# A two-layer hybrid backbone on one core: convolution taps issued during the attention of layer 1, second group's queries during the first, modulation vectors of layer 0 one place earlier

## The chip, the core and the metric

The kernel runs on one core of a Trainium2 chip as one program. Each engine works through its own list of instructions in order: TensorE (PE, matrix products and transposes), VectorE (DVE), ScalarE (ACT), GpSimd (POOL), and SyncE (SP), which issues the transfers. The metric is the device time of one execution in microseconds. Three runs of the kernel before took 1968.97, 1981.49 and 1981.51 us; the median is 1981.49 us.

## The reference, cut to what matters

Two layers; each has a token-mixing part and an MLP, with 512 latent tokens and 256 context tokens, width 1024, all in fp32. In the mixing part one projection feeds three mixers and 24 blocks of gates:

```python
ul_pool, ul_q, ul_k, ul_v, ul_conv, ul_gate = _split_in(hl @ w_in[i] + b_in[i])
ol = _latent_attention(ql, kl, vl, kc, vc, attn_sink[i])   # 8 heads in 2 groups, +-128 tokens and all context keys
y_conv = _conv_module(...)  # GLU -> depthwise conv, 31 taps -> LayerNorm -> swish -> product
g_pool, g_attn, g_conv = jnp.split(sigmoid(gates), N_BRANCH, axis=-1)
y = (g_pool * y_pool + g_attn * y_attn + g_conv * y_conv) @ w_out
```

The modulation vectors (shift, scale and gate, s = 0 to 5 of each layer) are `silu(c) @ w_mod + b_mod`. The context stream is updated in layer 0 only; in layer 1 the context gives keys and values and nothing else, so `has_ctx` is false there.

## The kernel before, in words

Every operand of a product is held as a high and a low part (`wh`/`wl`, `actah`/`actal`), and three products make one fp32-like product: L156 for stationary weights. A weight unit is 128x512: a transfer, a cast on ACT (L134) and a subtraction (L137) on POOL or DVE.

`w_phase` (L560) is the mixing part of one layer. Its work on PE comes from two sources that are merged while the program is written:

- `other = gated_steps()` is a generator of dense work: eight attention gates (stored to `sgd`), then for each of eight blocks of channels the pool gate with the pool branch's product and the conv gate with the conv branch's product; the sum of both goes to DRAM (`mfd`). `branch_steps` gives nothing (`None`) until its branch is in `mixed`. A gate's tanh is on ACT (L611), a branch's gating on DVE (L621).
- Work with chains of dependences (values, pool products, conv norm, blocks of attention) is put in a heap by `later(columns, steps)` and comes up when that many more columns of PE work were issued. `cover(columns)` issues that many columns of `other`. `pace(steps, every)` issues one step of a third stream each so many columns. When `other` gives `None`, the heap is drained with nothing between its pieces; `flush()` does the same.

Layer 1 in the kernel before: values, keys and the first group's queries; then `conv` (L312) puts 62 DVE taps (two halves of 128 channels by 31 taps, 512 tokens each) in one block, accumulating in one 1024-wide PSUM tile; then `cover(118000)`; then the pool products (L722) and `conv_norm` (L328: transposes, LayerNorm and swish in two blocks of 256 tokens), each waiting for cover; then attention, eight blocks (`items`, L756) of a group and 128 queries. A block makes scores on PE, the row maximum (L511, L512) on DVE, exp (L515) on ACT, scaling (L423) on DVE and one quarter on another engine, transposes on PE, high and low parts (`pth` L445 on ACT, `ptl` L446 on DVE) and the products with V. The second group's queries are made between block 4 and block 5. At the end the rest of `other` and the output loop (`fin`) run.

PSUM: `psa` (2 banks) is shared by the branch products, the attention outputs `po`, pool products and conv norm; `psg` (2 banks) by gates and projections; `pss` by the scores (two tiles of two banks).

Layer 0 has the same order with both streams, `cover(145000)` under the taps, and one pace in the mixing part: the modulation vector s=2, one step each 10000 columns, whose weights arrive in `mg` tiles. The vectors s=3 and s=4 are paced through the output loop, and what is left is issued after it with nothing beside it (L836). A step has four products L185; the last one adds a row on DVE (L222) and, for s=3 and s=4, makes two PE transposes (L234).

Of the kernel before, what the change touches and what calls it, by code (L numbers as in the profile page):

```python
# [10 lines left out]
F32 = mybir.dt.float32  # L11
F32R = mybir.dt.float32r
AF = mybir.ActivationFunctionType
ALU = mybir.AluOpType
# [55 lines left out]
W_CONV1 = 118000  # L70
# [7 lines left out]
def backbone(ctx: ExitStack, tc: tile.TileContext, I: dict, out: bass.AP):  # L78
# [233 lines left out]
    def conv(pool, psum, cvec, gls, st):  # L312

        n = TL if st == 0 else TC
        ps = psum.tile([P, 1024], F32, tag="S", name=uid("cp"))
        accs = []
        for j in range(2):
            gl, run = gls[j, st], ps[:, j * 512:j * 512 + n]
            acc = pool.tile([P, n], F32, tag=f"ca{st}", name=uid("ca"), bufs=2)
            V.tensor_scalar(out=run, in0=gl[:, 0:n], scalar1=cvec[:, j, 0:1], scalar2=cvec[:, j, 31:32],  # L320
                            op0=ALU.mult, op1=ALU.add)
            for k in range(1, CK):
                V.scalar_tensor_tensor(out=run if k < CK - 1 else acc, in0=gl[:, k:k + n],
                                       scalar=cvec[:, j, k:k + 1], in1=run, op0=ALU.mult, op1=ALU.add)
            accs.append(acc)
        return accs

    def conv_norm(pool, scratch, cvec, accs, st, dst):  # L328
# [4 lines left out]
        for b0 in range(0, n, 256):  # L333
            pt, pb = bank(), bank()
# [12 lines left out]
            yield W_CN  # L347
            for j in range(2):
# [62 lines left out]
    def softmax_pv(pp, pss, g, Pt, vtiles, negm, sums, V_, sink, dst, qsl):  # L411
# [42 lines left out]
        t1 = pp.tile([64, 4, P], F32, tag="t1", name=uid("t1"), bufs=1)  # L454
        S.copy(t1, po[64:128, :].rearrange("p (a q) -> p a q", a=4))
        ot = pp.tile([P, 2, P], F32, tag="ot", name=uid("ot"), bufs=2)
# [6 lines left out]
    def attn_ctx(pp, pss, g, nb, Q, KH, KL, V_, nsink, sink, dst):  # L463
# [3 lines left out]
        for a in range(4):  # L467
            o = s[:, a * 256:(a + 1) * 256]
            T.matmul(o, Q[a][:, qsl], KH[g][:, CS], start=True, stop=False)
            T.matmul(o, Q[a][:, qsl], KL[g][:, CS], start=False, stop=True)  # L470
# [15 lines left out]
    def attn_lat(pp, pss, g, n, Q, KH, KL, V_, nsink, sink, dst, masks):  # L486
# [10 lines left out]
        for a in range(4):  # L497
            s = pss.tile([P, 1024], F32, tag="S", name=uid("S"))
            q = Q[a][:, qsl]
# [60 lines left out]
    def w_phase(i, A, B, has_ctx, pre, todo):  # L560
# [5 lines left out]
        with ExitStack() as ph:  # L566
# [8 lines left out]
            mg = ph.enter_context(tc.tile_pool(name=f"mg{i}", bufs=4 if todo else 6, reuse_waits="tile"))  # L575
            sgd = [dram.tile([P, W], F32, tag=f"sg{i}{m}", name=uid("sgd")) for m in range(KD)]
            mfd = [dram.tile([P, W], F32, tag=f"mf{i}{m}", name=uid("mfd")) for m in range(KD)]
            mix = ph.enter_context(ExitStack())
# [14 lines left out]
            if todo:  # L593
                pace((x for s in todo for x in mod_steps(i, s, 0, D, lambda: mg.tile(
                    [P, W], F32, tag="sg", name=uid("wm"))[:, :512])), 10000, 20000)
# [28 lines left out]
            def gated_steps():  # L624
                for m in range(KD):
                    g = yield from gate_steps(m, 1)
                    nc.sync.dma_start(out=sgd[m], in_=g)

                w, d, e, ahead = {}, {}, {}, 0 if todo else 2
                for m in range(ahead):  # L630
                    d[m] = yield from gate_steps(m, 0)
                for m in range(KD + 1):
                    if m + ahead < KD:
                        d[m + ahead] = yield from gate_steps(m + ahead, 0)
                    if m < KD:
                        w[m] = weight_a(I["wbr"][i, m][:, 0:4 * P])
                        yield from branch_steps(w[m], (0, 1), 0, d[m], outs_all, side["bank"])
                    if m:
                        e = yield from gate_steps(m - 1, 2)
                        yield from branch_steps(w.pop(m - 1), (2, 3), 2, e, outs_all, side["bank"])  # L640
# [3 lines left out]
            mixed, side = set(), {"bank": psa}  # L644
# [11 lines left out]
            masks = kv.tile([P, 2, P], F32R, tag="masks", name=uid("masks"))  # L656
            KH = [kv.tile([P, TA], F32R, tag=f"kh{g}", name=uid("kh")) for g in range(NKV)]
            KL = [kv.tile([P, TA], F32R, tag=f"kl{g}", name=uid("kl")) for g in range(NKV)]
            V_ = kv.tile([P, 6, NKV, P], F32R, tag="V", name=uid("V"))

            def evac(ps, t):
                qf = kv.tile([P, TA], F32, tag="qf", name=uid("qf"))
                for st, p_ in enumerate(ps):
                    sl = (LS, CS)[st]
                    S.activation(qf[:, sl], p_, AF.Identity, bias=b_in[:, t:t + 1])
                return qf

            def query(Q, g, jj, temp):
                t = T_Q + 2 * g + jj
                qf = evac(proj(t, LC), t)  # L670
                rope(temp, qf, cs)
                for par in range(2):
# [3 lines left out]
                    V.tensor_copy(q[r, :W], qf[r, :W])  # L676
                    V.tensor_tensor(out=q[ro, :W], in0=qf[r, :W], in1=q[r, :W].bitcast(F32),
                                    op=ALU.subtract)
# [12 lines left out]
            vf = evac(proj(T_V, [LS, CS]), T_V)  # L691
# [14 lines left out]
            kf = evac(proj(T_K, [LS, CS]), T_K)  # L706
# [8 lines left out]
            Q = [kv.tile([P, W], F32R, tag=f"q{a}", name=uid("q")) for a in range(4)]  # L715
# [26 lines left out]
            accs = {st: conv(cp, pss, cvec, gls, st) for st, _ in outs_all}  # L742
            cover((W_CONV0 if has_ctx else W_CONV1) - W_PC)
            for wait in pool_products():
                cover(wait)
            mixed.add(0)
            cover(W_PC)
            flush()
            for st, _ in outs_all:
                for wait in conv_norm(cp, scratch, cvec, accs[st], st, B):  # L750
                    cover(wait)
            mixed.add(2)
            t12.close()
            pp = mix.enter_context(tc.tile_pool(name=f"pp{i}", bufs=1, side="right", reuse_waits="tile"))

            def items():  # L756
                for g in range(NKV):
                    if g:
                        Q[:] = [kv.tile([P, W], F32R, tag=f"q{a}", name=uid("q")) for a in range(4)]
                        for jj in range(2):  # L760
                            query(Q, g, jj, pp.tile([P, TL], F32, tag="rt", name=uid("rt"), bufs=1))
                    for n in range(4):
                        yield attn_lat(pp, pss, g, n, Q, KH, KL, V_, nsink, sink, B, masks)
# [49 lines left out]
            mixed.add(4)  # L813
            mix.close()
            if todo:
                for _ in pe["pace"]:
                    pass
            pace(None, 0)
# [3 lines left out]
            side["bank"] = psg  # L822
            if todo:
                pace((x for s in (3, 4) for x in mod_steps(i, s, 0, D, lambda: fin.tile(
                    [P, D], F32, tag="wm", name=uid("wm"), bufs=4))), 9000)
            drain(other)
            for m in range(KD):
# [4 lines left out]
                nc.sync.dma_start(out=d, in_=mfd[m])  # L832
# [236 lines left out]
    with tc.manual_schedule(engines={mybir.EngineType.PE}):  # L1069
# [159 lines left out]
```

## Time and profile before

| what | value |
|---|---|
| median of three runs | 1981.49 us |
| the profiled execution | 1975.67 us, its span 1973.9 us |
| PE busy | 1848.6 us, 94% of the span |
| DVE, POOL, ACT busy | 1200.3, 771.6, 730.8 us |
| mixing part of layer 1 | about 1232 to 1550 us |

A stretch of the windows view gives, for each engine, how much of that stretch it was busy, and the granted clock of TensorE as a share of full speed. A row of the waits view gives how long an engine stood idle before one line's instructions, and what ended it.

### The profile page before, as it was taken

What the parts mean: (1) busy time and instruction counts of PE and PEld (TensorE: products, weight loads), DVE (VectorE), ACT (ScalarE), POOL (GpSimd) and SP (SyncE); (2) the same over time, 40 slices, a digit from 0 to 9 for tenths busy, and PEclk for the clock granted to TensorE, in tenths of its full rate; (3) what the DMA queues carried; (4) which work ended last, traced back from release to release, by engine and by line L of the source; (5) the groups of instructions that cost most, each with busy time, mean ns of one, the idle gap of its engine ahead of it and who ended that gap; (6) DMA issues with size and microseconds to landing.
All of it is one profiled execution on the core that took longest, in us unless ns stands there. A gap on an engine that the chain in (4) does not pass through costs nothing. (4 is left out here: it accounts for less than half of the span.)

```text
span 1973.9 us, 27007 instructions
## 1 busy us (share of the span) xinstructions
PE 1848.6 (94%) x9910; PEld 1548.4 (78%) x9910; DVE 1200.3 (61%) x2067; ACT 730.8 (37%) x1359; POOL 771.6 (39%) x629
## 2 busy tenths in 40 slices
PE   6999899899899999999999988999988989999997
PEld 4788788787678888888788868777866768888886
DVE  6489655654478946865533584786575784333356
ACT  4432255353234422233133344434444354333331
POOL 3653432322434422222122546664342554333343
PEclk8999999999999999999999989999999989999999
DMA  8523111114865434464422423141212753332341
GB/s 304 176 90 118 62 59 46 53 44 154 281 219 190 161 112 133 155 213 143 146 62 86 129 96 105 61 149 63 69 65 96 260 189 118 96 96 86 107 129 43
DMA packets 117557, 244.94 MB, mean 124 GB/s; under 512 B 14608, under 2 KB 16944, under 8 KB 117424
## 3 DMA queue, kind: packets, MB, share of 16 engines
q1 hardware_dynamic: 117424, 243.21, 38.0%
q8 instruction: 78, 1.28, 0.3%
q14 instruction: 55, 0.45, 0.1%
HBM read 223.20 MB, written 19.96 MB: 123 GB/s over the span
## 5 line engine op out<-in xcount | busy, mean ns | idle before, releaser
L137 POOL TENSOR_TENSOR wl<-raw,wh 128x512 fp32r<-128x512 f32 x371 | 516.7, 1405 | 783.6 <-ACT wh L134 698.9
L134 ACT CAST wh<-raw 128x512 fp32r<-128x512 f32 x506 | 310.8, 621 | 596.0 <-PE ps L167 292.1
L156 PE MATMUL ps<-actbh,wh 128*128 128x512 f32 (+1 forms) x1016 | 353.4, 348 | 14.3 <-DVE sg L621 6.9
L156 PE MATMUL ps<-actbl,wh 128*128 128x512 f32 (+1 forms) x1016 | 348.3, 343 | 3.1 <-POOL actbl L251 3.1
L156 PE MATMUL ps<-actbh,wl 128*128 128x512 f32 (+1 forms) x1016 | 347.8, 342 | 2.7 <-DVE rs L261 1.3
L156 PE MATMUL ps<-actah,wh 128*128 128x512 f32 (+1 forms) x928 | 331.4, 357 | 13.7 <-ACT actah L248 4.7
L156 PE MATMUL ps<-actal,wh 128*128 128x512 f32 (+1 forms) x928 | 327.4, 353 | 3.3 <-DVE actal L1097 1.9
L156 PE MATMUL ps<-actah,wl 128*128 128x512 f32 (+1 forms) x928 | 326.9, 352 | 0.4 <-POOL wl L137 0.3
L156 PEld LDWEIGHTS ps<-actbh,wh 128*128 128x128 f32 x1016 | 194.5, 191 | 45.2 <-DVE sg L621 10.0
L156 PEld LDWEIGHTS ps<-actbh,wl 128*128 128x128 f32 x1016 | 194.4, 191 | 25.6 <-DVE wl L137 2.4
L156 PEld LDWEIGHTS ps<-actbl,wh 128*128 128x128 f32 x1016 | 194.6, 192 | 23.3 <-POOL actbl L251 3.8
L156 PEld LDWEIGHTS ps<-actah,wh 128*128 128x128 f32 x928 | 177.5, 191 | 43.8 <-ACT actah L248 5.1
L156 PEld LDWEIGHTS ps<-actal,wh 128*128 128x128 f32 x928 | 177.6, 191 | 25.6 <-DVE actal L1097 2.2
L156 PEld LDWEIGHTS ps<-actah,wl 128*128 128x128 f32 x928 | 177.4, 191 | 24.2 <-POOL wl L137 1.0
L165 PE MATMUL ps<-wh,actah 128*128 128x512 f32 x480 | 192.6, 401 | 2.2 <-DVE acc L977 2.0
L167 PE MATMUL ps<-wh,actal 128*128 128x512 f32 x480 | 190.5, 397 | 3.5 <-DVE actal L251 3.5
L166 PE MATMUL ps<-wl,actah 128*128 128x512 f32 x480 | 190.1, 396 | 0.0
L137 DVE TENSOR_TENSOR wl<-raw,wh 128x512 fp32r<-128x512 f32 x135 | 127.8, 947 | 99.9 <-ACT wh L134 97.3
L204 DVE SCALAR_TENSOR_TENSOR wm<-wm,sc,wm 128x512 f32<-128x512 f32 x140 | 124.4, 924 | 67.1 <-DMA wm<-in_wmod 67.0
L970 DVE TENSOR_TENSOR acc<-ps,acc 128x512 f32<-128x512 f32 x140 | 94.7, 684 | 95.3 <-PE ps L167 95.2
L165 PE MATMUL ps<-wh,actbh 128*128 128x512 f32 (+1 forms) x328 | 127.2, 388 | 1.5 <-DVE fg L621 1.5
L166 PE MATMUL ps<-wl,actbh 128*128 128x512 f32 (+1 forms) x328 | 126.8, 387 | 1.0 <-POOL wl L137 1.0
(207 smaller groups left out, 2721.7 us busy)
## 6 DMA issues: line engine op xcount, KB each, us to landing
raw<-in_w SPq DMA_DIRECT2D x264, 256.0 KB
raw<-in_win SPq DMA_DIRECT2D x154, 256.0 KB
wm<-in_wmod SPq DMA_DIRECT2D x72, 512.0 KB
raw<-in_wout SPq DMA_DIRECT2D x56, 256.0 KB
wm<-in_wmod SPq DMA_DIRECT2D x48, 256.0 KB
raw<-in_wbr SPq DMA_DIRECT2D x32, 256.0 KB
x1d<-R SPq DMA_DIRECT2D x10, 512.0 KB
acc<-in_b SPq DMA_DIRECT2D x10, 512.0 KB
```

The source lines that it names most:

```text
L134: S.copy(wh, r)
L137: e.tensor_tensor(out=wl, in0=r, in1=wh[:].bitcast(F32), op=ALU.subtract)
L156: T.matmul(ps, w(hl, w0 + n), x[xi][:, k, sl], start=(start and first and hl == 0 and xi == 0), stop=(stop and last and hl == 1))
L165: T.matmul(ps, x[0][:, k0 + k, tsl], wh, start=(k == 0), stop=False)
L166: T.matmul(ps, x[0][:, k0 + k, tsl], wl, start=False, stop=False)
L167: T.matmul(ps, x[1][:, k0 + k, tsl], wh, start=False, stop=(k == n - 1))
L204: V.scalar_tensor_tensor(out=o, in0=x, scalar=sc[:, k, r:r + 1], in1=o, op0=ALU.mult, op1=ALU.add)
L970: V.tensor_add(a, ps, a)
```

## The change: what it does

- Branch products take their bank from `psg` in both layers. `channels` replaces `evac(proj())`, with a bank and an evacuation for each slice.
- Layer 0: the paced stream of the mixing part holds s=2 and s=3 (and steps each 12000 columns), the output loop only s=4.
- Layer 1: the taps leave their solid block. After `cover(22000)` attention starts, the pool products come by `later`, and when they are done `pace(convolution(), 4000)` issues one tap each 4000 columns, each half in a `psa` bank of its own. Conv norm follows by `later`.
- Layer 1: `other` has eight attention gates, then eight pool gates with their branch products (stored to `mfd`), then eight conv gates with theirs, which read `mfd` back, add on POOL and store to `mf2`. The branch weights are loaded twice.
- Layer 1: the second group's queries are made ahead of blocks 2 and 3 of the first group, into the context columns of `B[0]`; V and the masks lie in those of `B[1]`.
- After attention the pace is drained and `flush()` is called.

```diff
-    def conv(pool, psum, cvec, gls, st):
+    def conv_steps(pool, banks, cvec, gls, st, accs):
         n = TL if st == 0 else TC
-        ps = psum.tile([P, 1024], F32, tag="S", name=uid("cp"))
-        accs = []
         for j in range(2):
-            gl, run = gls[j, st], ps[:, j * 512:j * 512 + n]
+            gl, run = gls[j, st], banks(j)[:, :n]
...
                 V.scalar_tensor_tensor(out=run if k < CK - 1 else acc, in0=gl[:, k:k + n],
                                        scalar=cvec[:, j, k:k + 1], in1=run, op0=ALU.mult, op1=ALU.add)
+                yield
...
+                if not has_ctx:
+                    for m in range(KD):
+                        g = yield from gate_steps(m, 0)
+                        w = weight_unit(I["wbr"][i, m][:, 0:4 * P])
+                        yield from branch_steps(lambda hl, k: w[hl][:, k * P:(k + 1) * P], (0, 1), 0, g,
+                                                outs_all, psg)
+                        nc.sync.dma_start(out=mfd[m], in_=g)
+                    for m in range(KD):
+                        e = yield from gate_steps(m, 2)
+                        w = weight_unit(I["wbr"][i, m][:, 0:4 * P])
+                        yield from branch_steps(lambda hl, k: w[hl][:, k * P:(k + 1) * P], (2, 3), 2, e,
+                                                outs_all, psg)
+                        g = mg.tile([P, W], F32, tag="sg", name=uid("sg"))
+                        nc.sync.dma_start(out=g, in_=mfd[m])
+                        G.tensor_tensor(out=g, in0=g, in1=e, op=ALU.add)
+                        nc.sync.dma_start(out=mf2[m], in_=g)
+                    return
...
+            def convolution():
+                accs = []
+                yield from conv_steps(cp, lambda j: bank(), cvec, gls, 0, accs)
+                later(W_CT, stages(conv_norm(cp, scratch, cvec, accs, 0, B), 2))
...
+                cover(W_QR)
+                later(W_PU, stages(pool_products(), 0))
...
+                        if not has_ctx and g == 0 and n in (1, 2):
+                            nq = nq or [B[0][:, 2 * a:2 * a + 2, CS] for a in range(4)]
+                            query(nq, 1, n - 1, rope_temp())
...
             mixed.add(4)
+            for _ in pe["pace"] or ():
+                pass
+            pace(None, 0)
+            flush()
             mix.close()
...
-                pace((x for s in (3, 4) for x in mod_steps(i, s, 0, D, lambda: fin.tile(
+                pace((x for s in todo[2:] for x in mod_steps(i, s, 0, D, lambda: fin.tile(
...
-            w_phase(i, A, B, not last, pre, () if i else (2,))
+            w_phase(i, A, B, not last, pre, () if i else (2, 3, 4))
```

**Place one: DVE in layer 1's attention of the changed kernel**, second half of block 3's scores. `mx` and `ngm` are the row maximum of a score tile `S`, `ps_12213` the taps' accumulator, `ca_12214` their result.

```order
L517 TENSOR_REDUCE mx_12490<-S_12547 128x1
L326 SCALAR_TENSOR_TENSOR ps_12213<-gl_11626,cvec_11573,ps_12213 128x512
L518 SCALAR_TENSOR_TENSOR ngm_12489<-mx_12490,nsink_11587 128x1
L326 SCALAR_TENSOR_TENSOR ps_12213<-gl_11626,cvec_11573,ps_12213 128x512 x3
L450 TENSOR_TENSOR ptl_12579<-pt_12569,pth_12578 128x512
L517 TENSOR_REDUCE mx_12490<-S_12586 128x1
L450 TENSOR_TENSOR ptl_12583<-pt_12569,pth_12582 128x512
L518 SCALAR_TENSOR_TENSOR ngm_12489<-mx_12490,nsink_11587 128x1
L326 SCALAR_TENSOR_TENSOR ps_12213<-gl_11626,cvec_11573,ps_12213 128x512
L326 SCALAR_TENSOR_TENSOR ca_12214<-gl_11626,cvec_11573,ps_12213 128x512
```

In the kernel before, the taps stood ahead of all attention on this engine:

```order
L323 SCALAR_TENSOR_TENSOR cp_11974<-gl_11602,cvec_11557,cp_11974 128x512 x13
L323 SCALAR_TENSOR_TENSOR ca_11975<-gl_11602,cvec_11557,cp_11974 128x512
L320 TENSOR_SCALAR cp_11974<-gl_11609,cvec_11557 128x512
L323 SCALAR_TENSOR_TENSOR cp_11974<-gl_11609,cvec_11557,cp_11974 128x512 x29
L323 SCALAR_TENSOR_TENSOR ca_12007<-gl_11609,cvec_11557,cp_11974 128x512
```

The taps now stand between the steps of attention, up to four in a row.

**Place two: PE at conv norm of layer 1.** `ca` are the convolution's results, `cn` their normalised form, `ps_13811` and `ps_12556` gates. In the changed kernel:

```order
L159 MATMUL ps_13811<-actbh,wl_13801 128x512
L341 MATMUL ps_13840<-ident_66,ca_12214 128x128
L341 MATMUL ps_13840<-ident_66,ca_13161 128x128
L341 MATMUL ps_13840<-ident_66,ca_12214 128x128
L341 MATMUL ps_13840<-ident_66,ca_13161 128x128
L355 MATMUL ps_13864<-ident_66,cn_13845 128x128 x4
L341 MATMUL ps_13883<-ident_66,ca_12214 128x128
L341 MATMUL ps_13883<-ident_66,ca_13161 128x128
L341 MATMUL ps_13883<-ident_66,ca_12214 128x128
L341 MATMUL ps_13883<-ident_66,ca_13161 128x128
L355 MATMUL ps_13907<-ident_66,cn_13888 128x128 x4
L159 MATMUL ps_13811<-actbh,wh_13800 128x512
```

In the kernel before, from the transposes of the first normalised block to those that open the second (21 and 21 products of gates and branches stand ahead of each L351):

```order
L351 MATMUL ps_12495<-ident_66,cn_12500 128x128 x4
L156 MATMUL ps_12556<-actbh,wh_12545 128x512
L156 MATMUL ps_12556<-actbl,wh_12545 128x512
L156 MATMUL ps_12556<-actbh,wl_12546 128x512
L156 MATMUL ps_12556<-actbh,wh_12545 128x512
L156 MATMUL ps_12556<-actbl,wh_12545 128x512
L156 MATMUL ps_12556<-actbh,wl_12546 128x512
L338 MATMUL ps_12587<-ident_66,ca_11975 128x128
L338 MATMUL ps_12587<-ident_66,ca_12007 128x128
L338 MATMUL ps_12587<-ident_66,ca_11975 128x128
L338 MATMUL ps_12587<-ident_66,ca_12007 128x128
L156 MATMUL ps_12556<-actbh,wh_12551 128x512
```

The two blocks of conv norm now stand back to back, behind the end of attention, with no product between transposes in and transposes out.

**Place three: DVE in layer 0, at the end of the taps.** `row` is the modulation vector s=3, `ca_1539` the last tap of the 512 latent tokens, `cp_1571` and `ca_1604` those of the context. In the changed kernel:

```order
L326 SCALAR_TENSOR_TENSOR cp_1506<-gl_746,cvec_700,cp_1506 128x512
L326 SCALAR_TENSOR_TENSOR cp_1571<-gl_956,cvec_700,cp_1571 128x256
L326 SCALAR_TENSOR_TENSOR ca_1539<-gl_746,cvec_700,cp_1506 128x512
L326 SCALAR_TENSOR_TENSOR cp_1571<-gl_956,cvec_700,cp_1571 128x256
L225 TENSOR_TENSOR row_2083<-ps_1668,row_2083 128x256
L326 SCALAR_TENSOR_TENSOR cp_1571<-gl_956,cvec_700,cp_1571 128x256
L253 CAST pwh_2227<-pw_2225 128x128
```

and on PE the transposes that need this row, inside a gate:

```order
L159 MATMUL ps_2070<-actal,wh_2025 128x256
L159 MATMUL ps_2070<-actah,wl_2026 128x256
L237 MATMUL ps_1668<-ident_66,row_2083 128x128 x2
L159 MATMUL ps_2070<-actah,wh_2031 128x256
L159 MATMUL ps_2070<-actal,wh_2031 128x256
```

Neither the row's addition nor these transposes stood in this part before. Between the transposes and the first pool product there are 41,472 columns of L159.

## Rows read from the trace of the kernel before

**Rows 1.** Costliest groups of the page: busy us, mean ns, idle before, releaser.

```profile
L156 PE MATMUL ps<-actbh,wh 128*128 128x512 f32 (+1 forms) x1016 | 353.4, 348 | 14.3 <-DVE sg L621 6.9
L137 POOL TENSOR_TENSOR wl<-raw,wh 128x512 fp32r<-128x512 f32 x371 | 516.7, 1405 | 783.6 <-ACT wh L134 698.9
```

**Rows 2.** Windows: stretch, length, busy us (instructions) of each engine, clock, DMA.

```profile
500.00:550.00 50.00, 42.56 (x274) 31.44 (x273) 22.84 (x31) 12.66 (x19) 22.10 (x14) 0.93 0.85 285
1240.00:1330.00 90.00, 86.86 (x403) 71.65 (x403) 76.22 (x105) 31.06 (x54) 58.24 (x46) 1.00 0.35 113
1330.00:1352.00 22.00, 17.46 (x76) 13.93 (x77) 13.33 (x31) 5.28 (x10) 11.10 (x13) 0.92 0.19 60
...
1400.00:1450.00 50.00, 41.98 (x214) 34.48 (x213) 31.20 (x54) 20.77 (x40) 22.87 (x19) 0.98 0.22 73
1450.00:1513.00 63.00, 60.02 (x306) 49.61 (x307) 40.19 (x81) 33.23 (x70) 18.17 (x14) 0.97 0.21 64
1513.00:1550.00 37.00, 30.56 (x131) 22.44 (x129) 24.72 (x33) 14.20 (x25) 18.54 (x14) 1.00 0.58 190
```

**Rows 3.** Waits of PE, 1400 to 1550 us: total us, times, longest.

```profile
PE S L501 <- DVE q L677: 5.5, 1, 5.5
PE ps L452 <- DVE ptl L446: 2.7, 7, 0.8
```

**Rows 4.** Timeline of DVE, layer 1: start us, length us, count.

```profile
1268.06 0.74 DVE L323 SCALAR_TENSOR_TENSOR cp<-gl,cvec,cp 128x512 f32<-128x512 f32 x1
1268.72 1.12 DVE L409 TENSOR_TENSOR qf<-qf,rt 128x512 f32<-128x512 f32 x1
...
1304.01 22.92 DVE L323 SCALAR_TENSOR_TENSOR cp<-gl,cvec,cp 128x512 f32<-128x512 f32 x29
```

**Rows 5.** Groups of DVE by shape, 1353 to 1513 us: busy us, mean ns.

```profile
L446 DVE TENSOR_TENSOR ptl<-pt,pth 128x512 fp32r<-128x512 f32 x31 | 21.4, 690 | 21.1 <-ACT pth L445 20.8
L511 DVE TENSOR_REDUCE mx<-S 128x1 f32<-128x640 f32 x16 | 13.1, 819 | 4.1 <-PE S L509 3.9
L512 DVE SCALAR_TENSOR_TENSOR ngm<-mx,nsink 128x1 f32<-128x1 f32 x32 | 10.0, 312 | 0.7
L423 DVE TENSOR_SCALAR P<-P,es 128x640 f32<-128x640 f32 x12 | 7.7, 697 | 0.1
...
L677 DVE TENSOR_TENSOR q<-qf,q 64x512 fp32r<-64x512 f32 x4 | 3.7, 931 | 0.1
...
L409 DVE TENSOR_TENSOR qf<-qf,rt 128x512 f32<-128x512 f32 x2 | 2.4, 1214 | 1.9 <-POOL rt L407 1.8
...
L676 DVE CAST q<-qf 64x512 fp32r<-64x512 f32 x4 | 2.1, 535 | 0.1
```

**Rows 6.** Timeline of conv norm in layer 1, DVE's start and PE's transposes.

```profile
1335.04 0.43 DVE L343 BATCH_NORM_STATS2 st<-ps 128x6 f32<-128x256 f32 x1 [2.27 <-PE ps L338]
1340.40 0.63 PE L351 MATMUL ps<-ident,cn 128*128 128x128 f32 x4 [0.61 <-DVE cn L345]
...
1342.90 0.43 DVE L343 BATCH_NORM_STATS2 st<-ps 128x6 f32<-128x256 f32 x1
...
1350.49 0.63 PE L351 MATMUL ps<-ident,cn 128*128 128x128 f32 x4 [2.84 <-DVE cn L345]
```

**Rows 7.** Groups of ACT, table loads.

```profile
L515 ACT ACT_TABLE_LOAD x2 | 2.6, 1283 | 1.7 <-DVE ngm L512 1.7
```

**Rows 8.** Waits of PE, 185 to 225 us.

```profile
PE ps L156 <- DVE sg L621: 2.5, 1, 2.5
PE ps L734 <- DVE pwh L250: 2.4, 1, 2.4
```

**Rows 9.** Waits of PE, 525 to 560 us.

```profile
PE ps L185 <- DMA wm<-in_wmod: 5.6, 3, 3.1
```

**Rows 10.** Timeline in layer 0 at the end of the taps, DVE and PE.

```profile
199.85 0.73 DVE L323 SCALAR_TENSOR_TENSOR ca<-gl,cvec,cp 128x512 f32<-128x512 f32 x1
204.59 0.39 PE L734 MATMUL ps<-actbh,pwh 128*128 128x512 f32 x1
...
205.05 0.39 PE L736 MATMUL ps<-actbh,pwl 128*128 128x512 f32 x1
```

More of the change, by code (lines that the diff above doesn't have):

```diff
@@ L593, in w_phase @@
             if todo:
[L594 to L595 removed]
+                pace((x for s in todo[:2] for x in mod_steps(i, s, 0, D, lambda: mg.tile(
+                    [P, W], F32, tag="sg", name=uid("wm"))[:, :512])), 12000, 20000)
             def proj(t, sls):
@@ L714, in w_phase, with queries @@
                                     in1=KH[g][r, :].bitcast(F32), op=ALU.subtract)
-            Q = [kv.tile([P, W], F32R, tag=f"q{a}", name=uid("q")) for a in range(4)]
+            def queries():
+                return [kv.tile([P, W], F32R, tag=f"q{a}", name=uid("q"))[:, :].rearrange(
+                    "p (b c) -> p b c", c=TC) for a in range(4)]
+            Q = queries()
             query(Q, 0, 0, scratch("rt")[:, :TL])
@@ L740, in pool_products, with stages @@
                         yield W_PP
[L742 to L750, printed above, removed]
-                    cover(wait)
-            mixed.add(2)
-            t12.close()
+            def stages(gen, branch):
+                yield 0
+                wait = next(gen, None)
+                if wait is None:
+                    mixed.add(branch)
+                    if branch == 0:
+                        pace(convolution(), EV_CONV)
+                else:
+                    later(wait, stages(gen, branch))
@@ new lines, in convolution @@
+            def convolution():
+                accs = []
+                yield from conv_steps(cp, lambda j: bank(), cvec, gls, 0, accs)
+                later(W_CT, stages(conv_norm(cp, scratch, cvec, accs, 0, B), 2))
+            if has_ctx:
+                accs = {}
+                for st, _ in outs_all:
+                    big = pss.tile([P, 1024], F32, tag="S", name=uid("cp"))
+                    accs[st] = []
+                    for _ in conv_steps(cp, lambda j: big[:, 512 * j:512 * j + 512], cvec, gls, st, accs[st]):
+                        pass
+                cover(W_CONV0 - W_PC)
+                for wait in pool_products():
+                    cover(wait)
+                mixed.add(0)
+                cover(W_PC)
+                flush()
+                for st, _ in outs_all:
+                    for wait in conv_norm(cp, scratch, cvec, accs[st], st, B):
+                        cover(wait)
+                mixed.add(2)
+                t12.close()
+            else:
+                cover(W_QR)
+                later(W_PU, stages(pool_products(), 0))
@@ L754, in w_phase, with rope_temp @@
             pp = mix.enter_context(tc.tile_pool(name=f"pp{i}", bufs=1, side="right", reuse_waits="tile"))
+            def rope_temp():
+                if not has_ctx:
+                    return scratch("rt")[:, :TL]
+                return pp.tile([P, TL], F32, tag="rt", name=uid("rt"), bufs=1)
             def items():
+                nq = None
                 for g in range(NKV):
                     if g:
-                        Q[:] = [kv.tile([P, W], F32R, tag=f"q{a}", name=uid("q")) for a in range(4)]
@@ L760, in items @@
-                        for jj in range(2):
-                            query(Q, g, jj, pp.tile([P, TL], F32, tag="rt", name=uid("rt"), bufs=1))
+                        Q[:] = nq or queries()
+                        if not nq:
+                            for jj in range(2):
+                                query(Q, g, jj, rope_temp())
                     for n in range(4):
+                        if not has_ctx and g == 0 and n in (1, 2):
+                            nq = nq or [B[0][:, 2 * a:2 * a + 2, CS] for a in range(4)]
+                            query(nq, 1, n - 1, rope_temp())
@@ L831, in w_phase @@
                 d = fin.tile([P, W], F32, tag="d", name=uid("fd"))
-                nc.sync.dma_start(out=d, in_=mfd[m])
+                nc.sync.dma_start(out=d, in_=mf2[m])
                 drain(branch_steps(w, (4, 5, 6, 7), 0, g, outs_all, psg))
```

76 lines of the change are left out of this document (42 added, 34 removed).

## The prediction

> **What bounds the kernel now.** I read the costliest groups of the page first, then windows by stage, then the waits of PE inside the stages that the change touches, then single instructions. PE carries the time: its work is the same before and after, so the question is only which waits of PE go and which come. The windows [rows 2] show where they are now. In layer 1 the stretch under the taps has PE at 86.86 of 90 us with DVE at 76.22; conv norm loses 4.5 of 22 us; attention loses 8.0 of 50 us around the second group's queries and 3.0 of the 63 behind them; its end loses 6.4 of 37 us. In attention DVE is busy 31.2 of 50 us: it has room, but less than half. In layer 0 PE loses 7.4 of the 50 us from 500 to 550, at a DMA share of 0.85.
>
> **What layer 1 can give.** Idle time of PE in the five stretches from 1240 us on [rows 2]: 3.1 + 4.5 + 8.0 + 3.0 + 6.4 = 25.1 us. The granted clock below 1.00 costs 22 x 0.08 + 50 x 0.02 + 63 x 0.03 = 4.7 us. So 29.8 us is all there is, if the new order leaves no wait in any of these places. For the largest single one, PE's 5.5 us for the second group's q [rows 3], the new place does away with it: these queries are now made two and three blocks ahead. The end of attention (2.7 us for `ptl` [rows 3] and the like) gets gates beside it, since eight conv gates are still unissued then. I take the whole 29.8 us off and price the new waits by themselves.
>
> **What the taps cost beside attention.** Of 62 taps, 31 stand between the first row maximum behind the pool products and the last one of block 3. One tap takes 0.66 us from its start to the next instruction's, and 22.92/29 = 0.79 us behind other taps [rows 4]; at 0.72 this is 22.3 us. Between the same two places DVE has eight maxima with their minima, 8 x (0.82 + 0.31) = 9.0; eight low parts, 8 x 0.69 = 5.5; six scalings of up to 0.70, 4.0; and two queries, 3.7 + 2.4 + 2.1 = 8.2 us by their three costliest lines [rows 5]. Lesser instructions I set against the overlap of neighbours. The sum is 49 us. PE has 161 products' worth of 512 columns there, by the order, at 0.23 us each (two steps take 0.46 us [rows 10]): 37.0 us. DVE comes out 12 us late, and PE waits for its maxima. For the other 31 taps: 22.3 + 11 x 1.13 + 10 x 0.69 + 4.0 = 45.6 us against 157.5 x 0.23 = 36.2, late by 9.4. Score tiles come in pairs, so some of it is borne. I take 11 us for the first half and 5 for the second, 16 in all. Lowest is 0 (the tiles bear it). Highest is 40, nine tenths of the 62 x 0.72 = 44.6 us of taps.
>
> **What conv norm costs at the end.** The order of the change has no product between the transposes in and the transposes out, for both blocks. So the whole chain of DVE and POOL lies on PE's path: 1340.40 - 1335.04 = 5.4 us and 1350.49 - 1342.90 = 7.6 us [rows 6], 13.0 together; before, 21 products (4.8 us) hid most of each. The swish behind it needs a table load that was not there, because exp has run since. It is 1.28 us [rows 7], and the five k-steps of a gate behind the last transposes (15 products, 3.4 us) hide most of the swish. I take 14 us; 11 if DVE, with nothing else to do, is quicker; 18 with load and swish exposed. The Trainium skill, page "ScalarE: Activation LUTs", section "What ACT_TABLE_LOAD costs", counts 2.66 us for a change of function set, about half of it a drain behind the load. The trace agrees with the load itself (1283 ns [rows 7]) and has no row for a drain; with that figure the sum would be 1.4 us higher.
>
> **The second loading of branch weights.** Eight more units, each a subtraction of 1.405 us on POOL [rows 1]. A block of conv gate and branch has three units, 4.2 us of POOL if all went there, under 30 products, 6.9 us. The loads stand two and more blocks ahead on SP; the store to `mf2` waits there for POOL's sum, but the weights behind it are for later blocks. Zero; if that cover went, 8 x 1.4 = 11 us.
>
> Layer 1: -29.8 + 16 + 14 = +0.2 us.
>
> **Layer 0.** With s=3 out of the output loop, the steps left at its end go. PE idles 7.4 us in 500 to 550, and the clock of 0.93 costs 3.5 [rows 2]; 5.6 us of the idle time is for the weights of these steps [rows 9]. I take 8.5 us off, between 5.6 and 10.9. But s=3 now ends inside the cover of the taps. Its row's addition stands on DVE behind the last tap of the latent tokens and one more: 200.6 [rows 10], plus about 0.7 for both. PE meets its transposes 41,472 columns, that is 81 x 0.23 = 18.6 us, ahead of the pool products, which began at 204.59 [rows 10]: at 186.0, and about 188 with 32 more products of s=3 (at most 0.12 each). **PE waits 13 us** for a vector that nothing needs until much later; 11 to 15 by that spread. The clock behind it: 1.8 us, as in the stretch of 1330 to 1352. PE then comes later to the pool products, while DVE does not, and its waits of 2.5 and 2.4 us [rows 8] go. 13 + 1.8 - 4.9 - 8.5 = +1.4 us. The 16 loads of s=3 move to a place with a light queue: the taps' stretch. Zero.
>
> **Banks.** Branch products leave the banks that attention uses; 6.9 us of PE's waits are for DVE's gating there [rows 1], 2.5 already counted. Now gates and branches share two banks, and can wait for one another. Between 4.4 us gained and as much lost, I take zero.
>
> **Sum:** +0.2 + 1.4 = +1.6 us, on the profiled execution's 1975.67 gives 1977.3. That execution stands 5.8 us below the median of the three runs, so against the median: **1983 us**, no change.
>
> **The rivals.**
> - *DVE keeps up (faster).* The taps fit into what attention leaves free: with 31.2 of 50 us busy, 18.8 are left, and the taps' 44.6 us in some 100 us of PE work need 22. Then the 16 us are 0; conv norm runs at its 11; banks give 4.4: 1983 - 16 - 3 - 4.4 = 1960 us. Against it: the order puts up to four taps in a row ahead of a maximum. The Trainium skill, page "Perfetto Trace Analysis", section "Optimization Strategy", says that interleaving stretches whose most contended engines differ may improve performance. The trace agrees that they differ (DVE 76.22 of 90 us under the taps, 31.2 of 50 in attention [rows 2]); by that rule this case is the likeliest.
> - *DVE becomes the bound of attention (slower).* Each tap in DVE's queue holds up the maximum that frees a score tile, then exp, the transposes and `ptl`, each of which comes back to DVE. It decides as soon as DVE's work between two maxima exceeds PE's there by more than the second score tile holds, 3500 columns or 1.6 us. Then the stall is 40 us and not 16: 2007 us. For it: 49 against 37 us in the first half, with the queries in it too. Against it: between the halves lie 124 products' worth (28.6 us) with no taps.
> - *The change does not do what it says in layer 0.* The end of the output loop keeps its wait for weights, since s=4 alone still comes late at this DMA share: 8.5 us more, 1992 us.
>
> **Chances and range.** My forecast, gains and new waits about equal: 0.5, own range 1970 to 1996 (stall 6 to 24, the rest as bounded). DVE keeps up: 0.25. DVE bounds: 0.2. No gain in layer 0: 0.05. A measurement of this kernel tells about 1% from no change, 20 us: faster is below 1961.7, slower above 2001.3. Faster has three fifths of its rival and a little of the forecast's edge, 0.20; slower most of its rival, 0.21; same 0.59. The range reaches to both rivals, 1957 to 2009.
>
> **What the profile after would show.** Right: a wait of PE of 10 us or more ahead of L237 near 188 us; two waits of 5 to 8 us ahead of L355 at the end of attention, with only transposes between; PE waiting for `mx` or `ngm` through the exps, or for `ptl`, in blocks 2 and 3, with DVE above 90% there; no wait for L188's weights at the end of layer 0's output loop; no wait for q ahead of block 5. Wrong: DVE under 85% while taps run, and scores that never wait; or gates found between the transposes of conv norm. The forecast fails most easily in the attention stall, whose bounds are 40 us apart.

## The result, and the profile after

The changed kernel took 1990.71 us (median of 8 runs, 1985.93 to 1994.2), the kernel before 1974.3 us in its 8 runs. The ratio is **1.007**, 95% interval 1.0054 to 1.0087: 0.7% slower, some 14 us. That is inside the range and inside the 1% called "no change", but on the slow side; the likeliest case was put at a change of +1.6 us.

Where it lies shows in three marks of the two profiled executions (spans 1973.9 and 1988.0 us). Layer 0's mixing part ends (first product of its output projection) at 543.2 us before and at 543.6 after. The parts behind each mixing part are as long as they were (650.2 and 650.0 us; 412.7 and 411.5 us). Layer 1's mixing part, from the last product of layer 0's MLP to the first of the output projection, took 356.8 and takes 371.5: **14.7 us, all of the difference between these two executions**. From the transposes of V (`vt`) to the first product of the output projection, a stretch that leaves the start of layer 1 out, it is 301.8 us before and 312.5 after; I call this *the stage* below. The other 4.0 us lie ahead of the stage (59.0 us against 55.0, at a granted clock of 0.88 against 0.94) and are not the change's: e_before_q below, whose program there is that of the kernel before, took 59.2 us for this stretch, and e_pace2500, with the changed program, 55.0. So the profiles put 10.7 us down to the change; the interval of the ratio is some 11 to 17 us.

The windows of the changed kernel, in the columns of [rows 2], and then the whole stage, after and before:

```profile
1240.00:1285.00 45.00, 41.52 (x195) 35.33 (x196) 28.04 (x39) 14.93 (x27) 28.73 (x22) 0.92 0.19 59
1285.00:1352.00 67.00, 53.20 (x245) 43.04 (x244) 55.17 (x96) 27.33 (x53) 29.61 (x25) 0.87 0.25 81
1352.00:1386.00 34.00, 33.93 (x179) 27.99 (x178) 21.57 (x44) 19.91 (x40) 11.21 (x10) 1.00 0.28 86
1386.00:1425.00 39.00, 33.94 (x178) 27.66 (x177) 37.94 (x69) 19.56 (x41) 12.33 (x11) 1.00 0.24 75
...
1472.00:1488.00 16.00, 6.49 (x27) 4.82 (x26) 9.55 (x32) 2.86 (x5) 4.27 (x7) 0.67 0.35 114
1488.00:1540.00 52.00, 52.00 (x223) 42.13 (x222) 16.70 (x22) 18.36 (x31) 24.17 (x20) 0.97 0.67 222
```

```profile
1252.60:1565.10 312.50, 281.45 (x1340) 229.07 (x1338) 216.97 (x376) 137.03 (x260) 134.47 (x110) 0.95 0.37 120
```

```profile
1248.40:1550.20 301.80, 277.85 (x1339) 226.51 (x1337) 215.43 (x364) 130.57 (x251) 141.31 (x114) 0.98 0.30 95
```

PE loses 13.8 of 67 us from the first scores through nearly all of the first 31 taps, 5.1 of 39 where most of the others run, nothing between them, and 9.5 of 16 us at conv norm. In the row of 1488 to 1540 us it is dense while DVE is busy a third of the time: gates that could have covered conv norm run there. DVE is at 82% in the second row and 97% in the fourth. Over the stage PE makes the same products; it idles 31.0 us where it had idled 24.0, and is busy 3.6 us longer at a lower granted clock (0.95 and 0.98).

What PE waits for there, from 1200 to 1300, 1300 to 1400 and 1400 to 1500 us (columns of [rows 3]; shorter waits left out):

```profile
PE S L507 <- ACT P L521: 5.8, 1, 5.8
...
PE ps L456 <- DVE ptl L450: 3.9, 2, 2.1
PE S L507 <- ACT P L521: 3.5, 3, 2.1
...
PE ps L355 <- DVE cn L348: 9.5, 4, 3.0
PE S L507 <- ACT P L521: 2.9, 3, 1.5
```

The wait for q [rows 3] is gone, as are those for `sg` and at the end of attention. Conv norm on PE reads so:

```profile
1473.39 0.60 PE L341 MATMUL ps<-ident,ca 128*128 128x128 f32 x4
1476.29 0.30 PE L355 MATMUL ps<-ident,cn 128*128 128x128 f32 x1 [2.30 <-DVE cn L348]
1478.21 0.90 PE L355 MATMUL ps<-ident,cn 128*128 128x128 f32 x3 [1.63 <-DVE cn L348]
1478.91 1.06 PE L341 MATMUL ps<-ident,ca 128*128 128x128 f32 x4
1482.59 0.45 PE L355 MATMUL ps<-ident,cn 128*128 128x128 f32 x1 [2.62 <-DVE cn L348]
1486.00 0.90 PE L355 MATMUL ps<-ident,cn 128*128 128x128 f32 x3 [2.97 <-DVE cn L348]
1487.13 0.63 PE L159 MATMUL ps<-actbl,wh 128*128 128x512 f32 x1
1487.55 0.63 PE L159 MATMUL ps<-actbh,wl 128*128 128x512 f32 x1
```

Transposes in, waits, transposes out, twice: 13 us in which there is no other product. The last two rows start 0.42 us apart where [rows 10] has 0.23: the granted clock is still at its lower level. The taps' results had been there for 38 us, since on DVE the last tap ended at 1435.3; what stands bare is conv norm, which the program puts behind attention:

```profile
1434.58 0.74 DVE L326 SCALAR_TENSOR_TENSOR ca<-gl,cvec,ps 128x512 f32<-128x512 f32 x1
```

### The profile page after: what moved, and what is told of

The parts are those of the page before. It is cut to its first block, busy times and chain, and to the rows that moved or that the text cites. A ratio compares the mean times of both kernels' runs of the same rounds, so it can differ in the third digit from the quotient of the medians.

```text
span 1988.0 us, 27115 instructions
## 1 busy us (share of the span) xinstructions
PE 1855.0 (93%) x9910; PEld 1552.9 (78%) x9910; DVE 1197.9 (60%) x2078; ACT 737.8 (37%) x1368; POOL 764.8 (38%) x626
## 3 DMA queue, kind: packets, MB, share of 16 engines
q8 instruction: 78, 1.28, 0.3%
## 5 line engine op out<-in xcount | busy, mean ns | idle before, releaser
L140 POOL TENSOR_TENSOR wl<-raw,wh 128x512 fp32r<-128x512 f32 x368 | 511.0, 1399 | 807.5 <-ACT wh L137 732.6
L137 ACT CAST wh<-raw 128x512 fp32r<-128x512 f32 x514 | 315.8, 622 | 624.8 <-PE ps L170 278.2
L159 PE MATMUL ps<-actbh,wh 128*128 128x512 f32 (+1 forms) x1016 | 354.8, 349 | 5.1 <-DVE rs L264 3.8
L159 PE MATMUL ps<-actbl,wh 128*128 128x512 f32 (+1 forms) x1016 | 350.3, 345 | 4.7 <-POOL actbl L254 4.6
L159 PE MATMUL ps<-actbh,wl 128*128 128x512 f32 (+1 forms) x1016 | 349.8, 344 | 2.7 <-DVE rs L264 1.3
L159 PE MATMUL ps<-actah,wh 128*128 128x512 f32 (+1 forms) x928 | 333.4, 359 | 13.7 <-ACT qf L695 3.2
L159 PE MATMUL ps<-actal,wh 128*128 128x512 f32 (+1 forms) x928 | 328.1, 354 | 2.2 <-POOL actal L254 1.3
L159 PE MATMUL ps<-actah,wl 128*128 128x512 f32 (+1 forms) x928 | 327.9, 353 | 0.4 <-POOL wl L140 0.3
L159 PEld LDWEIGHTS ps<-actbh,wh 128*128 128x128 f32 x1016 | 196.5, 193 | 32.6 <-issue 8.5
L159 PEld LDWEIGHTS ps<-actbh,wl 128*128 128x128 f32 x1016 | 196.2, 193 | 26.0 <-DVE wl L140 2.4
L159 PEld LDWEIGHTS ps<-actbl,wh 128*128 128x128 f32 x1016 | 196.7, 194 | 25.2 <-POOL actbl L254 5.4
L159 PEld LDWEIGHTS ps<-actah,wh 128*128 128x128 f32 x928 | 177.8, 192 | 47.6 <-issue 8.4
L140 DVE TENSOR_TENSOR wl<-raw,wh 128x512 fp32r<-128x512 f32 x146 | 136.9, 938 | 125.6 <-ACT wh L137 124.9
L159 PEld LDWEIGHTS ps<-actah,wl 128*128 128x128 f32 x928 | 178.1, 192 | 24.7 <-POOL wl L140 1.0
L159 PEld LDWEIGHTS ps<-actal,wh 128*128 128x128 f32 x928 | 178.2, 192 | 24.2 <-POOL actal L254 1.5
```

The source lines that it names most:

```text
L137: S.copy(wh, r)
L140: e.tensor_tensor(out=wl, in0=r, in1=wh[:].bitcast(F32), op=ALU.subtract)
L159: T.matmul(ps, w(hl, w0 + n), x[xi][:, k, sl], start=(start and first and hl == 0 and xi == 0), stop=(stop and last and hl == 1))
```

## The experiments

Three causes stood against each other: conv norm, uncovered since the taps' pace runs out; the taps, overloading DVE in attention; the moved queries or another part. Ratios are to the kernel before on the same chip, in parentheses the 95% interval; the stage is that of the one profiled execution. Whole times scatter by some us, so a single stage length is weaker than a ratio, and two ratios 0.3% (6 us) apart differ by about as much as their error. For the last kernel of the table no stage was read.

| kernel | ratio, interval | stage, us |
|---|---|---|
| before | 1 | 301.8 |
| changed | 1.0070 (1.0054 to 1.0087) | 312.5 |
| e_pace2500 | 1.0024 (1.0011 to 1.0038) | 305.3 |
| e_pace_qr | 1.0018 (0.9997 to 1.0038) | 304.0 |
| e_few_taps | 0.9996 (0.9975 to 1.0018) | 298.8 |
| e_q_early | 0.9997 (0.9972 to 1.0021) | 296.7 |
| e_q_cover | 0.9994 (0.9979 to 1.0008) | 299.0 |
| e_q_cover_taps | 0.9986 (0.9971 to 1.0001) | 298.9 |
| e_q_cover_few | 0.9967 (0.9953 to 0.9982) | 294.0 |
| e_qf_free | 1.0033 (1.0021 to 1.0045) | 304.6 |
| e_taps_solid | 1.0009 (0.9993 to 1.0024) | 299.8 |
| e_mods_back | 1.0059 (1.0039 to 1.0080) | 313.1 |
| e_before_q | 0.9994 (0.9978 to 1.0010) | 302.8 |
| e_before_banks | 1.0010 (0.9989 to 1.0032) | - |

**e_pace2500.**

```diff
-EV_CONV = 4000
+EV_CONV = 2500
```

> The changed kernel with one number changed: a tap each 2500 columns in place of 4000, so that the last tap is issued, and conv norm comes up, while attention still runs. Theory A (conv norm stands uncovered only because the taps' pace runs out after attention): its four waits ahead of L341 and L355 (9.5 us, 13.2 us with the slow products around them) shrink to 2 to 4 us, the attention stall grows by no more than 3 us since the scheduler issues the taps at about the same places; the time falls by 6 to 10 us against the changed kernel's 1990.7, to about 1982. Rival B (DVE's taps bound attention, and denser ones only move the loss): conv norm's waits go, but waits for row maxima, P and ptl in blocks 2 to 8 grow by as much; 1988 to 1994.

Theory A. 0.46% (9 us) of the loss went with one number. The waits for `cn` from 1400 to 1500 us fell from 9.5 to 0.5 us; of new ones only small sizes came, such as the first row:

```profile
PE ps L341 <- DVE cy L359: 1.7, 1, 1.7
...
PE ps L355 <- DVE cn L348: 0.5, 1, 0.5
```

**e_few_taps.** In e_pace2500, 58 of the 62 taps left out.

```diff
-            for k in range(1, CK):
+            for k in ks:              # ks=range(1, CK) where none is given
...
-                yield from conv_steps(cp, lambda j: bank(), cvec, gls, 0, accs)
+                yield from conv_steps(cp, lambda j: bank(), cvec, gls, 0, accs, (CK - 1,))
```

> A tap each 2500 columns, with the first and last tap of each half alone: 58 of layer 1's 62 taps are left out of the computation. Theory A (what PE waits for in attention is DVE behind the taps): the waits for P, ptl and maxima fall from 18 us to 5 or 6 and the time by 12 to 16 us against all taps, to 0.994 to 0.997 of the kernel before. Rival B (the waits belong to the chain of maximum, exp, scaling and transposes itself and to the queries): not more than 6 us less, 0.9995 to 1.002.

Rival B: 5.5 us less (with an error of some 5), where A wanted 12 to 16. Conv norm now stands in blocks 2 and 3, but the waits of PE there for P and `ptl`, 3.6 and 4.2 us with all taps, are still there without a tap (1300 to 1350 us, this kernel):

```profile
PE S L507 <- ACT P L521: 2.7, 2, 2.1
PE ps L456 <- DVE ptl L450: 2.4, 2, 1.8
```

and its DVE shows whose they are, the second row being a row maximum that is ready for use only when `ngm` follows:

```profile
1307.17 0.74 DVE L410 STREAM_SHUFFLE rt<-qf 128x512 f32<-128x512 f32 x1
1307.80 0.81 DVE L517 TENSOR_REDUCE mx<-S 128x1 f32<-128x640 f32 x1
1308.53 1.31 DVE L412 TENSOR_TENSOR qf<-qf,cs 128x512 f32<-128x512 f32 x1
1309.76 0.15 DVE L518 SCALAR_TENSOR_TENSOR ngm<-mx,nsink 128x1 f32<-128x1 f32 x1
1309.83 0.68 DVE L450 TENSOR_TENSOR ptl<-pt,pth 128x512 fp32r<-128x512 f32 x1
1310.43 0.68 DVE L413 TENSOR_TENSOR qf<-qf,rt 128x512 f32<-128x512 f32 x1
...
1311.37 0.85 DVE L707 CAST actah<-qf 64x512 fp32r<-64x512 f32 x2
1312.25 1.40 DVE L708 TENSOR_TENSOR actah<-qf,actah 64x512 fp32r<-64x512 f32 x2
1313.69 0.69 DVE L450 TENSOR_TENSOR ptl<-pt,pth 128x512 fp32r<-128x512 f32 x1
```

The rope of a query (L410 to L413) and its parts (L707, L708) stand between a maximum and its `ngm`, and between one `ptl` and the next.

**e_q_early.** In e_pace2500, both queries ahead of all attention, `query(nq, 1, 0)` and `query(nq, 1, 1)` before `cover(W_QR)` in place of blocks 2 and 3.

> A tap each 2500 columns, and the second group's two queries are made ahead of all attention, behind the first group's, so that blocks 2 and 3 carry taps but no queries. Theory A (queries and taps together overload DVE in blocks 2 and 3: 49 us of work beside 37 us of PE): the 16 us that PE loses from the first maxima to block 4 fall to 7 or 8 us; 0.997 to 0.999 of the kernel before. Rival B (the taps alone bound these blocks, since the column pace only moves them together): 14 us or more are still lost there, 1.001 to 1.003.

By the ratio 5 us less than e_pace2500, with an error as large; its interval reaches into A's range and into B's. By the rows Theory A: from 1300 to 1400 us the waits for P are 1.2 us (5.0 in e_pace2500) and for `ptl` none (4.2), with all taps there. A new wait takes part of it back (1240 to 1350 us):

```profile
PE ps L159 <- ACT qf L695: 10.0, 3, 8.6
```

**e_q_cover, e_q_cover_taps, e_q_cover_few.** Gates between those queries against the wait for qf; then the taps' pace from ahead of the queries, with `EV_CONV = 3000`; then the first with 58 taps left out. The first, against the changed kernel:

```diff
-W_QR = 22000
+W_QR = 16000
...
-EV_CONV = 4000
+EV_CONV = 1500
...
+                for jj, gap in enumerate((11000, 11000)):
+                    cover(gap)
+                    query(nq_early, 1, jj, scratch("rt")[:, :TL])
                 cover(W_QR)
```

> All queries ahead of attention, with 11,000 columns of gates ahead of each of the second group's two and 16,000 behind the last; a tap each 1500 columns at most. Theory A (the loss of blocks 2 and 3 is the queries' DVE work standing ahead of maxima, and the 8.6 us wait of the run before this was the single query buffer, which gates between the queries hide): the wait for qf falls from 10 us to 1 or 2, PE loses at most 10 us from 1285 to 1400; 0.994 to 0.997 of the kernel before, faster than both. Rival B (the wait comes back at the first maxima, or the taps, now denser, stall attention): 0.999 to 1.002.

Theory B: no gain over e_q_early. The longest wait for qf fell from 8.6 us to 5.2, and with the denser taps there are 5.2 us of waits for P and 2.3 for `ngm` from 1350 to 1470 us. Against e_pace2500 it is 0.30% (6 us) faster, clear of the error: with gates, queries and denser taps together.

> As the one before, but the taps' pace begins ahead of the second group's queries, a tap each 3000 columns. Theory A (DVE has room before attention, 28 of 45 us busy there, so taps put there cost nothing): 1 to 4 us less than with the taps behind the pool products: 0.992 to 0.996 of the kernel before. Rival B (the taps stand ahead of the queries' rope, which then holds up the first scores): 2 to 6 us more, 0.998 to 1.001.

Neither: 0.9986 is in B's range, but not 2 to 6 us more than the run before; the two intervals overlap, and this one just reaches 1. It is the fastest version with all the work in it, and not shown to beat the kernel before.

> All queries ahead of attention with gates between them, and 58 of layer 1's 62 taps left out of the computation. It prices the taps with the queries out of the way. Theory A (taps cost little beside attention: 9 us of waits in blocks 4 to 8 before): 5 to 9 us less than the same kernel with all taps. Rival B (the taps fit altogether once the queries are gone): less than 3 us. Rival C (DVE is bound by the taps): 12 us or more.

Theory A: 0.27%, 5.3 us with an error of some 4, about as in the other pair without taps (B's 3 us are not excluded, C's 12 are). So 58 of the 62 taps beside attention cost about 5 us.

**e_qf_free.** Queries evacuated into rotating scratch tiles (`scratch("qf")` in place of the single `qf`), gates of 8000 and 22000 columns, EV_CONV 1500.

> All queries ahead of attention, with 8,000 columns of gates between the second group's two and 22,000 behind the last; a tap each 1500 columns at most; and layer 1's queries are evacuated into the five rotating scratch tiles in place of the single query buffer. Theory A (the 5.3 to 8.7 us that PE waited for qf in the three runs before was that buffer): the wait goes or falls below 1.5 us, nothing takes its place, 0.993 to 0.997 of the kernel before, faster than both kernels. Rival B (DVE has four queries and the pool sums in a row there, and PE waits for it at the first maxima instead): 0.998 to 1.001.

Theory B, and worse than it: the wait for qf is gone, and 8 us for the first P came in its place (of 15.5 us for P in the stage), since queries stand on DVE up to the first maximum:

```profile
1310.51 1.82 DVE L708 CAST actah<-qf 64x512 fp32r<-64x512 f32 x2
1312.36 1.40 DVE L709 TENSOR_TENSOR actah<-qf,actah 64x512 fp32r<-64x512 f32 x2
1313.80 0.23 DVE L253 CAST pwh<-pw 128x128 fp32r<-128x128 f32 x1
1313.94 0.68 DVE L517 TENSOR_REDUCE mx<-S 128x1 f32<-128x512 f32 x1
```

The gates ahead of the second group's first query went too (none, where e_q_cover has 11,000 columns), so the run does not price the buffer by itself.

**e_pace_qr.** In e_pace2500, `W_QR = 45000` in place of 22000.

> A tap each 2500 columns, and attention of layer 1 starts after 45,000 columns of gates in place of 22,000. Theory A (the first scores come up while DVE is still at the rope of the second query, and the exp table is loaded on the same chain): PE's wait of 5.8 us for P near 1291 us falls below 1.5 us and the slow products behind it go, 5 to 7 us less than with 22,000 columns: 0.997 to 1.000 of the kernel before on the same chip. Rival B (the wait is the price of starting attention at all; it comes at the later place too, or the end of attention runs out of gates): 1.002 to 1.005.

Unclear by the ratio, 0.06% less than e_pace2500. The first wait for P fell from 5.8 to 1.8 us, and others came: 3.9 us for one P and 2.0 for an `ngm` from 1300 to 1400. So that wait can be taken away, but no run shows that the time falls with it.

**e_taps_solid.** The loop of `convolution()` run at once under `cover(110000)`, then pool products and conv norm under cover.

> The changed kernel with layer 1's 62 taps back in one block under cover (110,000 columns), then pool products and conv norm under cover, then attention; queries, banks, the second loading of branch weights and layer 0 stay as changed. Theory A (the taps beside attention and conv norm behind it make the whole loss of layer 1): the 24 us that PE loses from 1285 to 1352 and the 13 us of conv norm fall to what the kernel before had there (about 9 us around pool products and conv norm), and the early queries keep their gain of 7 us; the time is 1965 to 1972, below the kernel before. Rival B (the early queries or the second pass over the branch weights cost): 1978 to 1990.

Between them: 12 us less than the changed kernel, the stage 2 us shorter than before, no faster in all. Of A's gain 7.5 us were lost to a wait that, by the program's text, the new order of `other` makes: with the pool branch not yet `mixed` and one pool gate issued, there is no gate left to issue.

```profile
1335.46 0.80 PE L768 MATMUL ps<-actah,pwh 128*128 128x512 f32 x1 [7.48 <-DVE pwh L253]
```

**e_before_q.** The kernel before, with the queries in blocks 2 and 3.

> The kernel before with one part of the change alone: layer 1's queries of the second group are made ahead of blocks 2 and 3 of the first, into the context columns of the other activation buffer. Theory A (this part is a gain by itself, since attention without taps leaves DVE 37% idle): PE's wait of 5.5 us for q and the slow products behind it go, at most 2 us comes back in blocks 2 and 3; 1966 to 1970 against 1974.3. Rival B (the queries' 11 us of DVE work delay the maxima of blocks 2 and 3 by as much as the wait was): 1972 to 1977.

Theory B. PE's 5.5 us for q [rows 3] go; from 1353 to 1450 us it now waits 6.3 us for `ptl` and 3.2 for P, where it had waited 1.4 for P and none of note for `ptl`. The move by itself brings no gain that can be told.

**e_mods_back and e_before_banks.** Layer 0's vectors as before, in the changed kernel; the branch products' banks alone (`"bank": psg`), in the kernel before.

> The changed kernel with layer 0's modulation vectors as before: s=2 alone in the mixing part, a step each 10000 columns, s=3 and s=4 in the output loop. Theory A (layer 0's move is a trade: the 9 us at the end of the output loop come back, the waits of PE near 148 us and the slow products behind it go): within 2 us of the changed kernel, 1989 to 1993, layer 0's part ends within 1 us of where it did. Rival B (the early vectors cost more than they give): 1982 to 1986. Rival C (they gain): 1996 to 2001.

The ratio does not part A from B: 0.11% less than the changed kernel, with overlapping intervals (1982 to 1990 us at 1974.3 for the kernel before). Layer 0's mixing part ends at 542.9 us, 543.6 in the changed kernel, which speaks for A. The trade shows: from 500 to 560 us the first row is back (none for L188 in the changed kernel), and from 100 to 205 us, where the changed kernel has the second, it has no wait.

```profile
PE ps L188 <- DMA wm<-in_wmod: 5.1, 3, 4.1
```

```profile
PE ps L188 <- DMA wm<-in_wmod: 4.8, 1, 4.8
```

> The kernel before with one part of the change alone: the branch products take their PSUM banks from the pair that gates use, in both layers. Theory A (the waits for DVE's gating go, 6.9 us, and as much comes back between gates and branches): 0.998 to 1.002 of the kernel before. Rival B (a gain by itself): 0.9965 or less. Rival C (gates wait for branches): 1.003 or more.

Theory A: no change that can be told. Its waits were not read, so that some went and as much came back stays unshown.

## Why the prediction came out as it did

**Layer 0: +1.4 forecast, +0.4 measured, for another reason.** That the sum fits is luck: the 13 us wait of PE for the row of s=3, its largest term, did not come. DVE was where I put it, but PE was not:

```profile
198.38 0.42 DVE L225 TENSOR_TENSOR row<-ps,row 128x256 f32<-128x256 f32 x1
```

```profile
199.83 0.38 PE L237 MATMUL ps<-ident,row 128*128 128x128 f32 x2
```

PE came at 199.8 and not at 188. From V's transposes to the first pool product it took 115.6 us instead of 100.5: the steps of the vectors (L188) were busy 7.2 us more (9.8 and 2.6), and PE waited 4.8 us for a weight of s=3, with slower products behind it. I priced the 16 loads of s=3 at zero, "a place with a light queue". They stand in SP's queue behind other transfers that wait for engines:

```profile
142.58 0.33 SPq L101 DMA_DIRECT2D inv<-in_inv  x1
143.00 1.20 SPq L232 DMA_DIRECT2D gd<-row  x4
...
146.28 0.36 SPq L132 DMA_DIRECT2D raw<-in_win  x1
...
149.65 0.33 SPq L132 DMA_DIRECT2D raw<-in_win  x1
150.03 0.90 SPq L186 DMA_DIRECT2D wm<-in_wmod  x2
```

The load of `inv` goes out when DVE is done with the pool sums that read the last one (L404, until 142.55); in the kernel before it went at 142.13, with no load of s=3 behind it. The four stores of the row of s=2 follow, and then two weight loads that wait for POOL (L140).

```profile
153.42 1.07 PE L188 MATMUL ps<-wm,sc 128*32 128x256 f32 x4 [4.79 <-DMA wm<-in_wmod]
```

The end of the output loop gave what was forecast: no wait for L188 after 500 us, and PE idles 0.9 of the 50 us there instead of 7.4.

**Conv norm: 14 us forecast.** Right: 9.5 us of waits in 13 us without other products, in four waits where I named two, and 9 us of the whole time back with the pace changed. The cause was read from the order: 62 steps of 4000 columns and more do not end before attention does in the program, and conv norm, which follows them, is issued with nothing beside it, though DVE has run the last of them by then.

**The attention stall: 16 us forecast, right in size and wrong in its source.** In the two tap stretches PE idles 13.8 + 5.1 us on the windows, 5.8 of it the start of attention (next point), so 13 us, and slow products come behind them. I added up DVE's work against PE's and blamed the taps, with the queries along. Taken out, 58 taps give about 5 us in each of two pairs of runs. The queries out of blocks 2 and 3 take with them 8 us of waits for P and `ptl` there, with all taps in place (e_q_early), and in the kernel before they stall attention with no taps beside them. So the sum of DVE's work does not decide. That the place does, each instruction between a maximum and its `ngm` being waited for, is read from DVE's rows and not tested by a run of its own.

**The start of attention: not priced, 5.8 us and slow products behind it.** This step of the prediction failed: it has no term for it. With `cover(22000)` the first scores come while DVE is at the second query's rope, and the exp table is loaded on the same chain. Whether the wait costs its 5.8 us of time is open, since e_pace_qr takes 4.0 us of it away and others come. The rows:

```profile
1291.07 1.40 DVE L708 TENSOR_TENSOR q<-qf,q 64x512 fp32r<-64x512 f32 x2
1292.50 0.23 DVE L253 CAST pwh<-pw 128x128 fp32r<-128x128 f32 x1
1292.64 0.68 DVE L517 TENSOR_REDUCE mx<-S 128x1 f32<-128x512 f32 x1
1293.36 1.13 DVE L518 SCALAR_TENSOR_TENSOR ngm<-mx,nsink 128x1 f32<-128x1 f32 x1
```

```profile
1294.57 1.28 ACT L521 ACT_TABLE_LOAD   x1 [7.82 <-DVE ngm L518]
1295.86 0.69 ACT L521 ACTIVATE P<-S,ngm 128x512 f32<-128x512 f32 x1
```

```profile
1296.69 0.58 PE L507 MATMUL S<-kh,q 128*128 128x256 f32 x1 [5.77 <-ACT P L521]
```

The exp starts 0.01 us behind the end of the load, so 1.28 us are the whole price here. The Trainium skill, page "ScalarE: Activation LUTs", section "What ACT_TABLE_LOAD costs", counts 2.66 us for a switch; the trace agrees with the load's part of it and shows no more than that.

**"I take the whole 29.8 us off": the other step that failed.** Of the 29.8 us, 25.1 were idle time and 4.7 the clock. The idle time went for the most part: of the stage's 31.0 us of idle now, 28.4 are the waits named above (5.8 + 13.1 + 9.5), so 2.6 of the 24.0 us before are left, and some 21 went. The clock's 4.7 us did not come back: the same products took 3.6 us more. The new waits have low stretches of the clock behind them (0.87 around the start of attention, 0.67 at conv norm), and I had put a price on that in layer 0 alone. The terms then close: 5.8 + 13.1 + 9.5 - 21.4 + 3.6 = 10.6 us, where the stage took 10.7 more and I had +0.2. The largest misses are the clock (8.3 us) and the start of attention (5.8).

**Terms at zero.** The second loading of the branch weights shows no wait of PE in the stage, and the banks alone no change of the time.

**The rivals.** "DVE keeps up" failed: DVE's average room did not keep PE from waiting, since its order is fixed. Its premise was misread too: the busiest engine does not change between the taps' stretch and attention, it is PE in both (86.86 of 90 and 41.98 of 50 us [rows 2]). "DVE becomes the bound" holds for about 5 us of taps and not for 40. The 0.7% came by a sum of small sizes, none of them a rival of its own.

## What to carry to other kernels

An engine that is 60% busy on a chain of short steps is not free for the other 40%: two queries put into attention, with no taps beside them, brought as many waits as they took away. Ask what stands between a result and the one who waits for it, not how busy the engine is. A paced stream in the background has an end; count steps by columns against the stretch that covers it, since what follows the stream is bare if the cover ends first. A load in a queue stands behind every transfer ahead of it, and some of these wait for an engine: ask what they wait for, not how light the queue is. New waits bring slower products behind them: price both.

## What the runs showed of the hardware that was not expected

With four waits of only 1.6 to 3.0 us, one after the other, PE was busy 6.5 of the 16 us from 1472 to 1488; the granted clock of that stretch was 0.67, and the products behind it started 0.42 us apart, where two steps at the higher level (of 1.2 and 2.4 GHz) take 0.46 together. Before, with gates between the transposes, PE was busy 17.5 of 22 us around conv norm, and the clock was 0.92 [rows 2].
